# Up projection of a gated encoder block: products of a pair summed in one PSUM bank, next pair's first product moved forward

## The chip, the cores and the metric

The kernel runs on one core of a Trainium2 chip. The metric is device time in microseconds (us) of one execution. TensorE (PE) multiplies into PSUM banks; VectorE (DVE) and ScalarE (ACT) read PSUM; GpSimd (POOL) works on SBUF alone here; SyncE (SP) issues the DMAs. Each engine works through its own queue in order, and semaphores hold it until what it needs is done.

## The reference, cut to what matters

```python
h2 = _rmsnorm(x, norm2_g[l])
u = h2 @ ffn_up[l]                        # [2048, 1024] @ [1024, 5504]
u = cw[0] * _shift_prev(u) + cw[1] * u + cw[2] * _shift_next(u) + ffn_conv_b[l]
u_gate, u_val = jnp.split(u, 2, axis=-1)
x = x + (jax.nn.silu(u_gate) * u_val) @ ffn_down[l]
```

Everything ahead of this (two token mixers, merge, output projection) and behind it (down projection, last norm) is the same in both kernels. Float32 is needed all through, so a float32 factor is split into a high and a low part and a product takes three matmuls: high by high, high by low, low by high.

## The kernel before, in words

The up projection computes u transposed, channels on partitions and tokens along the row. The 5504 channels are 43 tiles of 128: 21 pairs of a gate tile and the value tile that goes with it, and one mixed tile of 64 and 64. The 2048 tokens go in two sweeps q = 0 and q = 1, of two blocks of 512 tokens each, so there are 42 pairs (line 1653 lists the steps; the mixed tile is the first step of sweep 0 and the last of sweep 1).

A pair is a product of 2 by 2 blocks: rows are the gate and the value tile, the inner index is the two halves of the 1024 inputs, columns are the two token blocks. It is done with seven block products in place of eight. On the weights' side stand A11, A12, A22 and the sums S1 to S4, on the activations' side B11, B21, B22 and the sums T1 to T4. `prod` (line 1491) does one block product: 4 slices of the inner index by 3 parts, 12 matmuls of 128x128 by 512 columns, into a bank of its own. `up_pair` (line 1620) calls it seven times, in the order A11·B11, S2·T2, S3·T3, S1·T1, A12·B21, A22·T4, S4·B22. ACT copies the first product into the tile row `ug` (line 1631); seven additions on DVE (`plus`, line 1498, a bank plus an SBUF row into an SBUF row) make the four quarters c11 and c12 (of `ug`) and c21 and c22 (of `uv`) out of it. Banks come from `bank()` (line 1574), eight in turn; `ug` and `uv` have two buffers each.

`pair_weights` (line 1550) makes the weights' side of the next pair while a pair runs. SP loads two raw tiles `rw` (line 1538), POOL forms the sums (line 1553, four of 128x512 a pair), ACT casts the high parts whi, s1h, s3h and s4h (line 226), and line 227 subtracts to get the low parts: wlo and s3l on POOL, s1l and s4l on DVE. The tiles whi and wlo have two buffers, the s tiles one each, so the next pair's S3 can be written only when A22·T4 of this pair is done. The raw tiles have four buffers, freed by s4l, s1l and s3l in turn.

`glu` (line 1602) is the convolution and gate of a pair that is finished: for two segments and both tiles one ACT operation (line 1597) and two DVE operations (lines 1598 and 1599), then SiLU on ACT (line 1605), a DVE multiplication (line 1607) and a DMA to `d_act`. It is called one step late, at the end of the loop at line 1656, through `pend`. `u_tile` and `u_done` move edge columns of the sweeps on POOL (lines 1585 to 1593).

In the last pair of sweep 0 (line 1662) the activations of sweep 1 replace those of sweep 0: `load_mat` (line 1541), called after each product, loads the operand that this product used last, through the single buffer `wraw` and the three buffers `ev`, and splits it anew. This stretch is called the turn below.

The order in each engine's queue is not written by hand: a scheduler lays it out at build time from a model of the durations, by priority, which is the order of the program; `tc.high_priority(300)` puts an instruction 300 places further ahead. On the chip this order is fixed.

Of the kernel before, what the change touches and what calls it, by code (L numbers as in the profile page):

```python
# [166 lines left out]
def _body(tc, A, out, dump=None, upto=99):  # L167
    nc = tc.nc
# [4 lines left out]
    def pool(stack, name, bufs=1, space=None, **kw):  # L173
        if space is None:
            return stack.enter_context(tc.tile_pool(name=name, bufs=bufs, **kw))
        return stack.enter_context(tc.tile_pool(name=name, bufs=bufs, space=space, **kw))
# [48 lines left out]
    def split(hi, lo, src, lo_eng=None, hi_eng=None):  # L225
        (hi_eng or nc.scalar.copy)(out=hi, in_=src)  # L226
        (lo_eng or nc.vector).tensor_tensor(out=lo, in0=src, in1=hi.bitcast(F32), op=ALU.subtract)  # L227
# [70 lines left out]
    def operand(b, q, **kw):  # L298
        t = [[q.tile([128, 4, BT], F32R, name=f"h{nm}{b}{i}", **kw) for nm in ("hi", "lo")] for i in range(2)]
        return [Halves([x[j] for x in t]) for j in range(2)]  # L300
# [3 lines left out]
    for b in range(NB):  # L304
        x_, y_ = operand(b, hb, **FOP) if b == NB - 1 else operand(b, hp)
# [93 lines left out]
    for b in range(NB):  # L399
        ps = pg.tile([128, 512], F32, name="pg", tag="pg")  # L400
# [3 lines left out]
        o = ev.tile([128, 512], F32, name="ev", tag="ev")  # L404
# [1007 lines left out]
    mats = {}  # L1412
# [12 lines left out]
    MATS = ("B11", "T2", "T3", "T1", "B21", "T4", "B22")  # L1425
# [64 lines left out]
    def prod(ps, *terms):  # L1490
        mm = [(w[ph == 2][:, k, :], x[ph == 1][:, k, :]) for w, x in terms for ph in range(3) for k in range(4)]
        for i, (w_, x_) in enumerate(mm):
            nc.tensor.matmul(ps, w_, x_, start=i == 0, stop=i == len(mm) - 1)  # L1493
        return ps

    def plus(o, ps, t):
        with tc.high_priority(300):
            nc.vector.tensor_tensor(out=o, in0=ps, in1=t, op=ALU.add)  # L1498

    def up_mixed(w, bank, u0, u1):  # L1500
        wh, wl = w
        a, b = (wh[:, 0:4], wl[:, 0:4]), (wh[:, 4:8], wl[:, 4:8])
        p1 = prod(bank(), (a, mats["B11"]))
        with tc.high_priority(300):
            nc.scalar.copy(out=u0, in_=p1)
        plus(u1, prod(bank(), (a, mats["T1"]), (b, mats["B22"])), u0)
        plus(u0, prod(bank(), (b, mats["B21"])), u0)
# [20 lines left out]
    fw = pool(s6, "fw", reuse_waits="tile")  # L1528
# [6 lines left out]
    def raw_tile(src):  # L1535
        r = fr.tile([128, 8, 128], F32, name="rw", tag="rw", bufs=4)
        if src is not None:
            sync.dma_start(out=f2(r), in_=src)
        return r

    def load_mat(n, i):
        r = wp.tile([128, 1024], F32, name="wraw", tag="wraw", bufs=1)
        sync.dma_start(out=r, in_=d_mat[i][:, 0:2, :].rearrange("p a b -> p (a b)"))
        split(f2(mats[n][0][:, 0:2, :]), f2(mats[n][1][:, 0:2, :]), r)
        for k in range(2, 4):
            r = ev.tile([128, BT], F32, name="ev", tag="ev")
            sync.dma_start(out=r, in_=d_mat[i][:, k, :])
            split(mats[n][0][:, k, :], mats[n][1][:, k, :], r, lo_eng=nc.gpsimd if k == 3 else nc.vector)

    def pair_weights(i):  # L1550
        r1, r2 = raw_tile(A["wup"][2 * i]), raw_tile(A["wup"][2 * i + 1])
        a, b = slice(0, 4), slice(4, 8)
        ps_ = lambda o, x, y, op: nc.gpsimd.tensor_tensor(out=o, in0=x, in1=y, op=op)  # L1553

        def parts(q, names, src, eng, n=8):
            h, l = [q.tile([128, n, 128], F32R, name=x, tag=x, bufs=2 if q is wp else 1) for x in names]
            split(f2(h), f2(l), f2(src), lo_eng=eng)
            return h, l

        h, l = parts(wp, ("whi", "wlo"), r1, nc.gpsimd)  # L1560
        w = {"A11": (h[:, a], l[:, a]), "A12": (h[:, b], l[:, b])}
        rs = raw_tile(None)
        ps_(rs[:, a], r2[:, a], r2[:, b], ALU.add)
        ps_(rs[:, b], rs[:, a], r1[:, a], ALU.subtract)
        h, l = parts(fw, ("s1h", "s1l"), rs, nc.vector)
        w["S1"], w["S2"] = (h[:, a], l[:, a]), (h[:, b], l[:, b])
        ps_(r2[:, a], r1[:, a], r2[:, a], ALU.subtract)
        h, l = parts(fw, ("s3h", "s3l"), r2, nc.gpsimd)
        w["S3"], w["A22"] = (h[:, a], l[:, a]), (h[:, b], l[:, b])
        ps_(r1[:, b], r1[:, b], rs[:, b], ALU.subtract)  # L1570
        w["S4"] = parts(fw, ("s4h", "s4l"), r1[:, b], nc.vector, 4)
        return w

    def bank():
        nbank[0] += 1
        return pus[(nbank[0] - 1) % 8 >= 3].tile([128, 512], F32, name="pu", tag="pu")


    COLS = ((slice(2, 514), slice(514, 1026)), (slice(1, 513), slice(517, 1029)))
    SEG = (((3, 511, 513), (514, 511, 1024)), ((1, 513, 0), (516, 513, 1535)))  # L1580

    def u_tile(q, m, tag):
        u = fu.tile([128, 1030], F32, name=tag, tag=tag, bufs=2)
        if q == 1:
            nc.gpsimd.memset(u[:, 0:1], 0.0)
            nc.gpsimd.tensor_copy(out=u[:, 513:517], in_=halo[:, m, :])
            nc.gpsimd.memset(u[:, 1029:1030], 0.0)
        return u

    def u_done(q, m, u):  # L1590
        if q == 0:
            nc.gpsimd.tensor_copy(out=halo[:, m, 0:2], in_=u[:, 2:4])
            nc.gpsimd.tensor_copy(out=halo[:, m, 2:4], in_=u[:, 1024:1026])

    def conv(m, u, c0, n):
        c = fc.tile([128, 513], F32, name="cv", tag="cv", bufs=6)[:, 0:n]
        nc.scalar.activation(out=c, in_=u[:, c0:c0 + n], func=AF.Identity, scale=vc("cw1", m), bias=vc("cb", m))  # L1597
        nc.vector.scalar_tensor_tensor(out=c, in0=u[:, c0 - 1:c0 - 1 + n], scalar=vc("cw0", m), in1=c, op0=ALU.mult, op1=ALU.add)  # L1598
        nc.vector.scalar_tensor_tensor(out=c, in0=u[:, c0 + 1:c0 + 1 + n], scalar=vc("cw2", m), in1=c, op0=ALU.mult, op1=ALU.add)  # L1599
        return c  # L1600

    def glu(q, i, ug, uv):
        for c0, n, t0 in SEG[q]:
            g = conv(2 * i, ug, c0, n)
            nc.scalar.activation(out=g, in_=g, func=AF.Silu)
            v = conv(2 * i + 1, uv, c0, n)
            nc.vector.tensor_tensor(out=v, in0=v, in1=g, op=ALU.mult)  # L1607
            sync.dma_start(out=d_act[i, :, t0:t0 + n], in_=v)
# [8 lines left out]
            sync.dma_start(out=d_act[21, 0:64, t0:t0 + n], in_=vm[0:64])  # L1617
            sync.dma_start(out=d_act[21, 64:128, t0:t0 + n], in_=vm[0:64])

    def up_pair(q, i, w, after):  # L1620
        ug, uv = u_tile(q, 2 * i, "ug"), u_tile(q, 2 * i + 1, "uv")
        c11, c12, c21, c22 = [u[:, c] for u in (ug, uv) for c in COLS[q]]

        def pr(a, b):
            ps = prod(bank(), (w[a], mats[b]))
            after(b)
            return ps

        p1 = pr("A11", "B11")
        with tc.high_priority(300):  # L1630
            nc.scalar.copy(out=c11, in_=p1)
        plus(c12, pr("S2", "T2"), c11)
        plus(c21, pr("S3", "T3"), c12)
        p5 = pr("S1", "T1")
        plus(c12, p5, c12)
        plus(c22, p5, c21)
        plus(c11, pr("A12", "B21"), c11)
        plus(c21, pr("A22", "T4"), c21)
        plus(c12, pr("S4", "B22"), c12)
        u_done(q, 2 * i, ug)  # L1640
        u_done(q, 2 * i + 1, uv)
        return lambda: glu(q, i, ug, uv)

    def mixed(q, w):
        u = u_tile(q, 42, "ug")
        if q == 0:
            nc.scalar.copy(out=u[:, 2:1026], in_=u42)
        else:
            up_mixed(w, bank, *[u[:, c] for c in COLS[q]])
        u_done(q, 42, u)  # L1650
        return lambda: glu_mixed(q, u)

    steps = [(0, 21)] + [(q, i) for q in range(2) for i in range(21)] + [(1, 21)]
    weights = lambda i: load_w(A["wup"][42]) if i == 21 else pair_weights(i)
    nw, pend = None, None
    for n, (q, i) in enumerate(steps):
        w = nw
        if n + 1 < len(steps):
            nw = weights(steps[n + 1][1])
        if n == 0:  # L1660
            load_mat("T4", 7)
        turn = q == 0 and i == 20
        if i == 21:
            fin = mixed(q, w)
        else:
            fin = up_pair(q, i, w, lambda b: load_mat(b, MATS.index(b)) if turn else None)
        if pend:
            pend()
        pend = fin
    pend()  # L1670
    s6.close()
# [97 lines left out]
    nx = prep_act(*work[0])  # L1769
    for tt in range(4):  # L1770
        fin = last_norm(tt, ps0[tt])
        next(fin)
        next(fin)
    for w, (tt, k0) in enumerate(work):
        ah, al = nx
        if k0 == 0:
            ps = banks(tt)
            fin = last_norm(tt, ps)
        if w + 1 < len(work):
            nx = prep_act(*work[w + 1])  # L1780
# [38 lines left out]
```

## Time and profile before

| | |
|---|---|
| median of 3 runs | 3625.32 us (3624.73 to 3634.07) |
| profiled execution, its own time | 3635.12 us |
| its span, first to last instruction | 3633.3 us |
| mean granted clock of TensorE | 0.956 |
| busy share of the span | PE 91%, DVE 64%, ACT 43%, POOL 28% |
| up projection, pairs and mixed tile | from about 2263 to 3140 us of the span |

The busy shares are means over stages with different limits. A matmul is recorded longer than the time by which it advances the next one, since they are pipelined; the pace of PE is read from starts of like instructions, and what holds it from the time that stands in brackets before an instruction.

### The profile page before, as it was taken

Reading aid. Unit: us, or ns where it says so; the run is one execution under the profiler, and the core shown is the slowest. Engines: PE = TensorE matmul, PEld = TensorE weight load, DVE = VectorE, ACT = ScalarE, POOL = GpSimd, SP = SyncE. Lnnn points to the kernel's source line nnn. Section 1 sums busy time; section 2 is a strip of 40 time slices with the busy share of each in tenths; the row PEclk is TensorE's granted clock in tenths of the full one; section 3 lists DMA queues with packets and bytes.
Section 4 is the critical chain, followed back from the end, with each engine's and each line's share of the span. In section 5 each row is a group of like instructions: output and inputs, shape, how many; then the busy total and the mean of one; then the engine's idle time right before and its main releaser. Section 6 shows DMA issues by size and latency. Waiting matters only on the chain. (4 is left out here: it accounts for less than half of the span.)

```text
span 3633.3 us, 58213 instructions
## 1 busy us (share of the span) xinstructions
PE 3291.2 (91%) x22232; PEld 2622.3 (72%) x22232; DVE 2319.6 (64%) x3913; ACT 1569.8 (43%) x2870; POOL 1003.0 (28%) x789
## 2 busy tenths in 40 slices
PE   7999999998978878877767899999989999999999
PEld 6787778766657666666655788877768777778887
DVE  5207764688846665666766466989899989724222
ACT  4214443555546666666544333434344443511111
POOL 1122222244430000000024412676766666100000
PEclk9999999999988999998988999999989999999999
DMA  4233444688883545555788746322232222523222
GB/s 148 91 118 109 134 137 134 197 224 229 230 247 108 158 151 158 153 182 177 216 244 271 286 140 199 115 76 79 78 125 96 81 76 82 168 86 115 83 83 64
DMA packets 403223, 531.30 MB, mean 146 GB/s; under 512 B 61504, under 2 KB 250560, under 8 KB 402944
## 3 DMA queue, kind: packets, MB, share of 16 engines
q1 hardware_dynamic: 402944, 527.58, 46.5%
q8 instruction: 175, 2.87, 0.3%
q14 instruction: 104, 0.85, 0.1%
HBM read 345.02 MB, written 181.93 MB: 145 GB/s over the span
## 5 line engine op out<-in xcount | busy, mean ns | idle before, releaser
L1553 POOL TENSOR_TENSOR rw<-rw 128x512 f32<-128x512 f32 x168 | 274.4, 1653 | 4.6 <-DVE cv L1598 1.2
L1706 PE MATMUL pd<-wdh,whi 128*128 128x512 f32 x672 | 261.6, 391 | 1.6 <-DVE ug L1498 1.6
L1707 PE MATMUL pd<-wdl,whi 128*128 128x512 f32 x672 | 261.4, 389 | 0.0
L1708 PE MATMUL pd<-wdh,wlo 128*128 128x512 f32 x672 | 259.3, 389 | 0.0
L241 PE MATMUL pg<-hhi,whi 128*128 128x512 f32 x928 | 249.0, 403 | 3.1 <-ACT whi L226 3.1
L241 PE MATMUL pg<-hlo,whi 128*128 128x512 f32 x928 | 250.5, 402 | 0.0
L241 PE MATMUL pg<-hhi,wlo 128*128 128x512 f32 x928 | 248.7, 403 | 0.0
L1073 POOL TENSOR_TENSOR Lt<-Lt,rnr 128x512 f32<-128x512 f32 x16 | 19.4, 1234 | 824.9 <-DVE rnr L254 766.5
L241 PEld LDWEIGHTS pg<-hhi,whi 128*128 128x128 f32 x928 | 176.2, 192 | 54.4 <-issue 14.3
L241 PEld LDWEIGHTS pg<-hhi,wlo 128*128 128x128 f32 x928 | 176.1, 192 | 49.8 <-issue 13.6
L241 PEld LDWEIGHTS pg<-hlo,whi 128*128 128x128 f32 x928 | 174.0, 191 | 52.4 <-issue 17.5
L227 POOL TENSOR_TENSOR wlo<-wraw,whi 128x1024 fp32r<-128x1024 f32 x46 | 114.9, 2498 | 349.6 <-PE pg L241 157.8
L1213 PE MATMUL pf<-fop,whi 128*128 128x512 f32 x576 | 172.6, 438 | 39.1 <-ACT whi L226 23.6
L1597 ACT ACTIVATE cv<-ug,vec 128x511 f32<-128x511 f32 (+1 forms) x88 | 71.9, 817 | 249.5 <-DVE ug L1498 249.5
L226 ACT CAST whi<-wraw 128x1024 fp32r<-128x1024 f32 x114 | 119.3, 1046 | 114.3 <-PE pg L241 50.8
L1213 PEld LDWEIGHTS pf<-fop,whi 128*128 128x128 f32 x576 | 113.7, 207 | 71.6 <-ACT whi L226 28.5
L1695 ACT CAST whi<-wraw 128x1024 fp32r<-128x1024 f32 (+1 forms) x36 | 35.2, 979 | 265.9 <-PE pd L1707 180.5
L1706 PEld LDWEIGHTS pd<-wdh,whi 128*128 128x128 f32 x672 | 126.1, 188 | 30.7 <-issue 5.0
L1598 DVE SCALAR_TENSOR_TENSOR cv<-ug,vec,cv 128x511 f32<-128x511 f32 (+1 forms) x88 | 125.0, 1421 | 35.8 <-ACT cv L1597 35.8
L227 DVE TENSOR_TENSOR wlo<-wraw,whi 128x1024 fp32r<-128x1024 f32 x68 | 83.7, 1231 | 99.4 <-ACT whi L226 98.8
L1708 PEld LDWEIGHTS pd<-wdh,wlo 128*128 128x128 f32 x672 | 126.2, 188 | 26.2
L1707 PEld LDWEIGHTS pd<-wdl,whi 128*128 128x128 f32 x672 | 126.2, 188 | 25.6
(470 smaller groups left out, 8274.4 us busy)
## 6 DMA issues: line engine op xcount, KB each, us to landing
rw<-wup SPq DMA_DIRECT2D x84, 512.0 KB, 3.5
wraw<-win SPq DMA_DIRECT2D x74, 512.0 KB, 4.1
Lt<-d_lt SPq DMA_DIRECT2D x64, 512.0 KB, 5.6
d_lt<-arbk SPq DMA_DIRECT2D x96, 256.0 KB, 3.9
d_gate<-ev SPq DMA_DIRECT2D x64, 256.0 KB, 3.5
X<-d_vt SPq DMA_DIRECT2D x64, 256.0 KB, 4.6
bj<-d_lt SPq DMA_DIRECT2D x128, 128.0 KB, 3.9
d_m<-ev SPq DMA_DIRECT2D x64, 256.0 KB, 5.4
```

The source lines that it names most:

```text
L226: (hi_eng or nc.scalar.copy)(out=hi, in_=src)
L227: (lo_eng or nc.vector).tensor_tensor(out=lo, in0=src, in1=hi.bitcast(F32), op=ALU.subtract)
L241: nc.tensor.matmul(ps, (wh, wh, wl)[ph], (xh, xl, xh)[ph], start=(ph == 0 and i == 0), stop=(ph == 2 and i == n - 1))
L1073: nc.gpsimd.tensor_tensor(out=y8[t], in0=y8[t], in1=b8(rr[:, t * 8:t * 8 + 8]), op=ALU.mult)
L1213: nc.tensor.matmul(ps, (wh, wh, wl)[ph][:, k0 + k, :], (hi, lo, hi)[ph][:, k, :], start=i == first[u] and k == 0, stop=i == last[u] and k ...
L1553: ps_ = lambda o, x, y, op: nc.gpsimd.tensor_tensor(out=o, in0=x, in1=y, op=op)
L1597: nc.scalar.activation(out=c, in_=u[:, c0:c0 + n], func=AF.Identity, scale=vc("cw1", m), bias=vc("cb", m))
L1598: nc.vector.scalar_tensor_tensor(out=c, in0=u[:, c0 - 1:c0 - 1 + n], scalar=vc("cw0", m), in1=c, op0=ALU.mult, op1=ALU.add)
L1695: nc.scalar.copy(out=ah[:, 0:n], in_=raw[:, 0:n])
L1706: nc.tensor.matmul(ps, a, wdh[k][:, cs], start=(k == 0), stop=False)
L1707: nc.tensor.matmul(ps, a, wdl[k][:, cs], start=False, stop=False)
L1708: nc.tensor.matmul(ps, l, wdh[k][:, cs], start=False, stop=False)
```

## The change

`up_pair` sums the partial sums in the bank. Bank X takes A11·B11, then S2·T2, S1·T1 and S4·B22 on top of it, and after each of the four ACT copies what X then holds: c11, c21, c22 and c12. Bank Y takes S3·T3 and later A22·T4; Z takes A12·B21. Three DVE additions are left: Y to c22, Z to c11, Y to c21. The first product of a pair and its copy (`up_head`) are called from the pair before, between A12·B21 and A22·T4 (`mid`), and so is the convolution of the pair before that (`pend`). The low part s3l is made on DVE.

```diff
-        h, l = parts(fw, ("s3h", "s3l"), r2, nc.gpsimd)
+        h, l = parts(fw, ("s3h", "s3l"), r2, nc.vector)
...
+    def add_to(ps, w, x, first=False):
+        mm = [(w[ph == 2][:, k, :], x[ph == 1][:, k, :]) for ph in range(3) for k in range(4)]
+        for n, (w_, x_) in enumerate(mm):
+            nc.tensor.matmul(ps, w_, x_, start=first and n == 0, stop=n == len(mm) - 1, skip_group_check=True)
+
+    def taken(o, ps):
+        with tc.high_priority(300):
+            nc.scalar.copy(out=o, in_=ps)
+
+    def up_head(q, i, w, after):
         ug, uv = u_tile(q, 2 * i, "ug"), u_tile(q, 2 * i + 1, "uv")
+        X = bank()
+        add_to(X, w["A11"], mats["B11"], True)
+        after("B11")
+        taken(ug[:, COLS[q][0]], X)
+        return ug, uv, X
+
+    def up_pair(q, i, w, after, st, mid):
+        ug, uv, X = st
         c11, c12, c21, c22 = [u[:, c] for u in (ug, uv) for c in COLS[q]]
...
-        p1 = pr("A11", "B11")
-        with tc.high_priority(300):
-            nc.scalar.copy(out=c11, in_=p1)
-        plus(c12, pr("S2", "T2"), c11)
-        plus(c21, pr("S3", "T3"), c12)
-        p5 = pr("S1", "T1")
-        plus(c12, p5, c12)
-        plus(c22, p5, c21)
-        plus(c11, pr("A12", "B21"), c11)
-        plus(c21, pr("A22", "T4"), c21)
-        plus(c12, pr("S4", "B22"), c12)
+        pr(X, "S2", "T2")
+        taken(c21, X)
+        Y = bank()
+        pr(Y, "S3", "T3", True)
+        pr(X, "S1", "T1")
+        taken(c22, X)
+        Z = bank()
+        pr(Z, "A12", "B21", True)
+        plus(c22, Y, c22)
+        plus(c11, Z, c11)
+        nx = mid()
+        pr(Y, "A22", "T4")
+        plus(c21, Y, c21)
+        pr(X, "S4", "B22")
+        taken(c12, X)
...
+    def between(n):
+        if pend:
+            pend()
+        if n + 1 < len(steps) and steps[n + 1][1] < 21:
+            return up_head(*steps[n + 1], nw, afters(n + 1))
...
         if i == 21:
             fin = mixed(q, w)
+            st = between(n)
         else:
-            fin = up_pair(q, i, w, lambda b: load_mat(b, MATS.index(b)) if turn else None)
-        if pend:
-            pend()
+            fin, st = up_pair(q, i, w, afters(n), st, lambda: between(n))
         pend = fin
```

## Rows read from the trace of the kernel before

**Rows 1.** Busy time by stretch: 16 pairs, the turn's 2, then 4, then 15 pairs

```profile
core 0: us, PE busy (x) PEld busy (x) DVE busy (x) ACT busy (x) POOL busy (x), PEclk, DMA share, GB/s
2360.37:2684.48 324.11, 310.88 (x1345) 249.87 (x1344) 293.53 (x303) 130.43 (x178) 226.46 (x164) 1.00 0.23 78
2684.48:2750.56 66.08, 49.20 (x169) 36.71 (x168) 59.93 (x57) 32.78 (x44) 40.90 (x38) 0.79 0.50 162
2750.56:2826.72 76.16, 76.16 (x337) 63.06 (x336) 70.24 (x77) 30.56 (x41) 49.59 (x50) 1.00 0.26 87
2826.72:3127.65 300.93, 290.48 (x1262) 235.18 (x1260) 271.89 (x290) 123.50 (x166) 183.27 (x173) 1.00 0.24 77
```

**Rows 2.** Timeline: end of a pair's last product on PE, its addition on DVE

```profile
2302.34 1.07 PE L1493 MATMUL pu<-mB22h,s4l 128*128 128x512 f32 x4
...
2309.78 0.68 DVE L1498 TENSOR_TENSOR ug<-pu,ug 128x512 f32<-128x512 f32 x1
...
2340.42 1.07 PE L1493 MATMUL pu<-mB22h,s4l 128*128 128x512 f32 x4
...
2350.37 0.68 DVE L1498 TENSOR_TENSOR ug<-pu,ug 128x512 f32<-128x512 f32 x1
...
2501.12 1.07 PE L1493 MATMUL pu<-mB22h,s4l 128*128 128x512 f32 x4
...
2512.60 0.68 DVE L1498 TENSOR_TENSOR ug<-pu,ug 128x512 f32<-128x512 f32 x1
```

**Rows 3.** Who waited for whom, 2400 to 2660 us: total, times, longest

```profile
ACT cv L1597 <- DVE ug L1498: 93.3, 26, 3.7
...
ACT cv L1605 <- DVE cv L1599: 45.4, 12, 3.8
DVE cv L1598 <- ACT cv L1597: 23.0, 26, 0.9
...
PE pu L1493 <- POOL s3l L227: 10.9, 13, 0.9
```

**Rows 4.** Timeline of one pair in sweep 0: how s3l comes late

```profile
2498.40 1.07 PE L1493 MATMUL pu<-mT4h,s3l 128*128 128x512 f32 x4
...
2506.32 1.03 ACT L226 CAST s3h<-rw 128x1024 fp32r<-128x1024 f32 x1
...
2507.91 2.38 POOL L227 TENSOR_TENSOR s3l<-rw,s3h 128x1024 fp32r<-128x1024 f32 x1
...
2510.34 1.20 PE L1493 MATMUL pu<-mT3h,s3l 128*128 128x512 f32 x4 [0.84 <-POOL s3l L227]
...
2513.80 0.74 DVE L1599 SCALAR_TENSOR_TENSOR cv<-ug,vec,cv 128x511 f32<-128x511 f32 x1
2513.88 5.21 POOL L1553 TENSOR_TENSOR rw<-rw 128x512 f32<-128x512 f32 x3
...
2514.46 1.78 DVE L1598 SCALAR_TENSOR_TENSOR cv<-ug,vec,cv 128x511 f32<-128x511 f32 x1
```

**Rows 5.** Groups by shape over ten pairs of sweep 0, 2400 to 2602.7 us

```profile
L1498 DVE TENSOR_TENSOR ug<-pu,ug 128x512 f32<-128x512 f32 x40 | 27.3, 683 | 1.0
L227 POOL TENSOR_TENSOR s3l<-rw,s3h 128x1024 fp32r<-128x1024 f32 x10 | 23.8, 2380 | 0.0
L227 DVE TENSOR_TENSOR s1l<-rw,s1h 128x1024 fp32r<-128x1024 f32 x10 | 12.2, 1216 | 0.0
L1631 ACT COPY ug<-pu 128x512 f32<-128x512 f32 x10 | 5.7, 565 | 0.0
```

**Rows 6.** The same groups in sweep 1, ten pairs, 2866.5 to 3067.34 us

```profile
L227 DVE TENSOR_TENSOR s1l<-rw,s1h 128x1024 fp32r<-128x1024 f32 x10 | 23.4, 2342 | 0.0
```

**Rows 7.** Timeline of the turn: B11's first cast, PE's longest wait, the last operand

```profile
2677.01 1.04 ACT L226 CAST mB11h<-wraw 128x1024 fp32r<-128x1024 f32 x1
...
2712.92 2.07 PE L1493 MATMUL pu<-mT1l,s1h 128*128 128x512 f32 x4 [7.29 <-DVE mT1l L227]
...
2732.29 2.70 DVE L227 TENSOR_TENSOR mB22l<-wraw,mB22h 128x1024 fp32r<-128x1024 f32 x1 [0.20 <-ACT mB22h L226]
```

**Rows 8.** Who waited for whom in sweep 1, 2800 to 3080 us

```profile
ACT cv L1605 <- DVE cv L1599: 86.8, 28, 5.5
```

More of the change, by code (lines that the diff above doesn't have):

```diff
@@ L1618, in glu_mixed, with pr @@
             sync.dma_start(out=d_act[21, 64:128, t0:t0 + n], in_=vm[0:64])
-    def up_pair(q, i, w, after):
-        ug, uv = u_tile(q, 2 * i, "ug"), u_tile(q, 2 * i + 1, "uv")
+    def add_to(ps, w, x, first=False):
[6 more added lines that the diff above has]
+    def up_head(q, i, w, after):
+        ug, uv = u_tile(q, 2 * i, "ug"), u_tile(q, 2 * i + 1, "uv")
+        X = bank()
[5 more added lines that the diff above has]
+        ug, uv, X = st
         c11, c12, c21, c22 = [u[:, c] for u in (ug, uv) for c in COLS[q]]
-        def pr(a, b):
-            ps = prod(bank(), (w[a], mats[b]))
+        def pr(ps, a, b, first=False):
+            add_to(ps, w[a], mats[b], first)
             after(b)
-            return ps
-        p1 = pr("A11", "B11")
-        with tc.high_priority(300):
-            nc.scalar.copy(out=c11, in_=p1)
-        plus(c12, pr("S2", "T2"), c11)
-        plus(c21, pr("S3", "T3"), c12)
-        p5 = pr("S1", "T1")
-        plus(c12, p5, c12)
-        plus(c22, p5, c21)
-        plus(c11, pr("A12", "B21"), c11)
-        plus(c21, pr("A22", "T4"), c21)
-        plus(c12, pr("S4", "B22"), c12)
+        pr(X, "S2", "T2")
[13 more added lines that the diff above has]
+        taken(c12, X)
         u_done(q, 2 * i, ug)
         u_done(q, 2 * i + 1, uv)
-        return lambda: glu(q, i, ug, uv)
+        return (lambda: glu(q, i, ug, uv)), nx
     def mixed(q, w):
@@ L1654, in _body, with afters @@
     weights = lambda i: load_w(A["wup"][42]) if i == 21 else pair_weights(i)
-    nw, pend = None, None
+    nw, pend, st = None, None, None
+    def afters(n):
+        turn = steps[n] == (0, 20)
+        return lambda b: load_mat(b, MATS.index(b)) if turn else None
+    def between(n):
[3 more added lines that the diff above has]
+            return up_head(*steps[n + 1], nw, afters(n + 1))
     for n, (q, i) in enumerate(steps):
@@ L1661, in _body @@
             load_mat("T4", 7)
-        turn = q == 0 and i == 20
         if i == 21:
             fin = mixed(q, w)
+            st = between(n)
         else:
-            fin = up_pair(q, i, w, lambda b: load_mat(b, MATS.index(b)) if turn else None)
-        if pend:
-            pend()
+            fin, st = up_pair(q, i, w, afters(n), st, lambda: between(n))
         pend = fin
```

## The prediction

> **What bounds the kernel now.** I read the busy time by stretch first. In the four pairs after the turn PE is busy all the time, and a pair takes 76.16 / 4 = 19.04 us [rows 1]. That is PE's floor, since the change keeps the seven products of 12 matmuls; one product is 19.04 / 7 = 2.72 us. The 16 pairs of the first long stretch take 20.26 us each and the 15 of the last 20.06 us [rows 1], so 16 x 1.22 + 15 x 1.02 = 19.5 + 15.3 = 34.8 us lie above the floor. The turn with its two pairs takes 66.08 us, 28.0 above.
>
> What makes the difference is seen in the timeline [rows 2]. A pair's last product ends on PE at 2303.41 us (start plus duration) and is added on DVE 6.4 us later; two pairs on the delay is 8.9 us, and at 2502 us it is 10.4. Between the first two of these PE made two pairs in 38.08 us and DVE in 40.59. So DVE runs its own circuit of 20.3 us whether PE is ahead or not, PE ran ahead as far as the buffers allow, and then took DVE's pace. In that circuit DVE is busy 293.53 / 16 = 18.35 us [rows 1] and waits 23.0 / 13 = 1.77 us for ACT's convolution operation [rows 3].
>
> The table of waits then shows where PE feels it: at s3l, up to 0.9 us a pair on the matmul itself [rows 3]. The chain in one pair [rows 4]: A22·T4 ends at 2499.47, but ACT casts s3h only at 2506.32, because it stands in its queue behind a convolution that waits up to 3.7 us for a DVE addition [rows 3]; POOL needs 2.38 us for s3l, and PE waits for its end. The late s3l is a symptom of a late DVE.
>
> **The change part by part.**
>
> *Additions to copies.* Seven additions become three: 4 x 0.683 = 2.73 us leave DVE a pair [rows 5]. ACT makes four copies in place of one, 3 x 0.565 = 1.70 us [rows 5]; it goes from 130.43 / 16 = 8.15 to 9.85 us of a 19.04 us pair. As load that is free; its place in the queue is the second rival.
>
> *s3l on DVE.* 2.38 us leave POOL [rows 5], whose load falls from 14.15 to 11.8 us a pair. DVE's price for the same shape is s1l: 1.22 us in sweep 0 [rows 5], 2.34 in sweep 1 [rows 6]; these are also the bounds, and I take each sweep's own. Freed POOL time helps DVE: the same kind of convolution operation takes 0.74 us beside an idle POOL and 1.78 beside a busy one [rows 4]. A 2.38 us s3l can hit none or two of them, so the relief lies between 0 and 2.1 us; I take 1.0.
>
> DVE's circuit becomes 20.26 - 2.73 + 1.22 - 1.0 = 17.8 us in sweep 0 and 20.06 - 2.73 + 2.34 - 1.0 = 18.7 in sweep 1. The dearest case is 20.26 - 2.73 + 2.34 = 19.9, the cheapest 16.4. Below 19.04 PE sets the pace, and the 34.8 us go.
>
> The Trainium skill (SBUF — State Buffer, Who interferes with whom) has VectorE instructions with two SBUF inputs and GpSimd instructions that read SBUF exclude each other for a whole instruction. The 0.74 and 1.78 us rows [rows 4] agree. By that rule s3l, which has two SBUF inputs, still takes its turn against POOL from the other side, and the circuit would stand at the dear end, the first rival.
>
> *One bank for four products.* X may be added to only after ACT has copied it. Between S2·T2 and S1·T1 stands one product, so c21's copy has 2.72 - 0.565 = 2.15 us to spare. c22's copy has three products or more of cover. c11's has two (A22·T4 and S4·B22 of the pair before) but needs a free buffer of `ug`, so the convolution of the pair before last must be done; DVE's former delay of 10.4 us is no longer affordable, and with DVE below the floor it does not build up. Y is read twice by DVE, with three products between its two fillings. I cost these waits together at 0.25 us a pair, between 0 and 1.0: 31 x 0.25 = 8 us.
>
> *What the moved head and convolution bring along.* The head's 12 matmuls pass A22·T4 and S4·B22 on PE. That takes 2.72 us from the time for the new S3: from the end of A22·T4 to S3·T3 there were three products, 8.16 us, now two, 5.44. s3h came 6.85 us late and lasts 1.03 [rows 4]; unchanged, it would cost PE 2.4 us a pair. I cost it at nothing, because the ACT wait that delayed it was for a late DVE addition. On POOL the head's edge columns wait for a free `ug`, and the next pair's sums queue behind them; the 2.38 us taken off POOL cover that. On SP the convolution's two stores stand earlier and wait for their multiplications, with the raw weight loads behind; those run a pair ahead. Costed at nothing; without that cover they would come out at PE like a late s3h.
>
> *The turn.* Seven operands pass one buffer, from B11's cast at 2677.01 to the end of B22's at 2734.99 [rows 7], 8.3 us each, with PE waiting up to 7.29 us for one. B11's three DMAs, casts and subtractions are now called two products, 5.4 us, ahead of the rest of the last pair, so the series may start that much sooner. B11 is also wanted two products sooner. I take -5 us, between -10 and +8. The first pair of all has no product between its head and S2·T2: +1 us.
>
> *Sum.* -19.5 - 15.3 + 8 - 5 + 1 = -31 us. The profiled execution took 3635.1 us, so 3604; the median of the runs stands 9.8 us below it, so 3594 on its level.
>
> **The rivals.**
>
> *DVE stays the bound.* s3l costs 2.34 us everywhere and relieves nothing: a circuit of 19.9 us gains 0.4 us a pair, 31 x 0.4 = 12 us in all and nothing in the turn: 3613. For it speaks the dear s1l of sweep 1; against it, s1l at 1.22 in sweep 0 in every one of ten pairs.
>
> *PE waits for ACT (slower).* The queue on ACT is fixed at build time, and a copy of X can come to stand behind a SiLU that waits for DVE's last convolution operation: 3.8 us once a pair in sweep 0 [rows 3], up to 5.5 in sweep 1 [rows 8]. Less the 2.15 us to spare, that is 1.7 to 3.4 us of idle PE a pair, and a late s3h would cost 2.4 in the same manner. At 2.4 us over 40 pairs it is 96 - 34.8 - 5 = +56 us: 3681. It decides from 40 / 40 = 1.0 us a pair on; below that the change still gains. For it: today each product has a bank of its own, and eight banks absorbed 10 us of delay that X cannot. Against it: those waits are long because DVE is late, and its load falls by a tenth.
>
> The Trainium skill (PSUM — Partial Sum Buffer, PSUM bank collisions raise a hardware error) says that TensorE must not write a bank while another engine reads it. Thus a copy in the middle of a sum is always time that X is closed to PE. No run here shows such a copy yet; by that rule alone this rival has its mechanism.
>
> *The order is not as written.* The scheduler may leave the head behind S4·B22. Then S2·T2 follows A11·B11 in the same bank, every pair waits for a copy of 0.565 us and two handoffs, some 1 us, and the gain is eaten: 3625.
>
> **How the numbers follow.** Forecast 0.52, DVE still the bound 0.18, PE waiting for ACT 0.18, order 0.12. The predicted time is the forecast's 3594 us. Its own range, with waits of 0 to 0.6 us a pair and the turn from -10 to +8, is 3580 to 3618. The whole range reaches from 3576 to 3638: the upper end takes in both middle cases and stalls of up to 1.3 us a pair, and leaves out most of the slower case. A measurement of this kernel can tell some 0.3%, 11 us, from no change. The first rival lies on that line and is halved; of the last one a quarter goes to slower: faster 0.61, same 0.18, slower 0.21.
>
> **What the profile would show.** If right: starts of like matmuls 19.04 to 19.3 us apart in both sweeps, no PE wait for s3l, DVE's busy share below 95% of a pair with three additions and one s3l more, additions on DVE within some 5 us of their product. The first rival would show a pair above 19.7 us with DVE without idle time. The second would show PE waiting ahead of S1·T1 or S2·T2 for ACT's copy, or ahead of S3·T3 for s3h, and under that row ACT waiting for DVE. The third would show A11·B11 directly ahead of S2·T2. The prediction is wrong if PE's idle time a pair is above 1 us, or if the turn costs over 8 us more.

## The result and the profile after

The changed kernel takes 3647.07 us (median of 4 runs, 3646.54 to 3650.16) against 3627.57 us (3624.73 to 3634.07) for the kernel before in the same series: a ratio of 1.0053 [1.0036, 1.007] (behind a ratio stand the ends of its 95% interval). The forecast was 3594 us with a range up to 3638. So the change made the kernel 0.5% slower where the forecast had it faster.

The profiled execution spans 3648.3 us at a mean granted clock of 0.953, against 3633.3 us at 0.956. Of these +15.0 us, 13.6 lie in the up projection: from its first matmul to the first of the down projection it takes 876.9 us before and 890.5 after. PE's floor for its 3576 matmuls, by the 19.04 us for the 84 matmuls of a pair [rows 1], is 3576 x 19.04 / 84 = 810.6 us.

The first part of the page, after:

```profile
PE 3296.5 (90%) x22232; PEld 2631.5 (72%) x22232; DVE 2233.4 (61%) x3787; ACT 1637.4 (45%) x2996; POOL 903.8 (25%) x747
```

The work went where it was meant to go: DVE's share fell from 64 to 61%, POOL's from 28 to 25%, ACT's rose from 43 to 45%. DVE is no longer the bound, and the time is longer all the same. Busy time by stretch, after: eight pairs of sweep 0, eight of sweep 1, and 3.51 us out of the first stretch, from where PE resumes after a long wait.

```profile
core 0: us, PE busy (x) PEld busy (x) DVE busy (x) ACT busy (x) POOL busy (x), PEclk, DMA share, GB/s
...
2411.65:2575.44 163.79, 155.33 (x673) 127.12 (x672) 127.80 (x129) 78.46 (x112) 90.31 (x72) 0.98 0.24 78
...
2915.79:3079.76 163.97, 156.23 (x673) 127.50 (x672) 131.32 (x129) 78.38 (x113) 84.34 (x89) 0.98 0.24 78
...
2514.99:2518.50 3.51, 3.51 (x8) 2.80 (x9) 1.80 (x2) 0.43 (x1) 0.18 (x1) 0.50 0.49 141
```

672 matmuls are eight pairs, so a pair takes 163.79 / 8 = 20.47 us in sweep 0 and 20.50 in sweep 1, where it took 20.26 and 20.06 before [rows 1]. DVE is busy 127.80 / 8 = 16.0 us of it, which leaves it 4.5 us idle a pair. PE is idle for 163.79 - 155.33 = 8.46 us in the eight pairs, and over these 3.51 us its granted clock is 0.50, the lower of its two levels (1.2 GHz).

Who PE waited for, after, from 2260 to 3160 us (total us, times, longest):

```profile
PE pu L1624 <- ACT s1h L226: 29.5, 10, 7.3
PE pu L1624 <- ACT ug L1628: 6.4, 1, 6.4
PE pu L1624 <- ACT uv L1628: 4.2, 4, 1.7
PE pu L1624 <- ACT s3h L226: 3.5, 1, 3.5
```

The waits for s3l [rows 3] are gone. In their place stand a few long waits for ACT. Five of them, of 6.05 to 7.26 us, come one in every eight pairs (at 2351, 2515, 2680, 2855 and 3019 us), always ahead of S2·T2, and half clock follows each. The third falls in the turn. One of them in the timeline, after:

```profile
2498.62 1.05 ACT L226 CAST s3h<-rw 128x1024 fp32r<-128x1024 f32 x1 [5.81 <-issue]
...
2499.49 0.69 DVE L1498 TENSOR_TENSOR uv<-pu,uv 128x512 f32<-128x512 f32 x1 [4.70 <-PE pu L1624]
...
2501.83 1.78 DVE L1598 SCALAR_TENSOR_TENSOR cv<-uv,vec,cv 128x511 f32<-128x511 f32 x1
...
2503.62 5.20 POOL L1553 TENSOR_TENSOR rw<-rw 128x512 f32<-128x512 f32 x3
...
2504.20 1.78 DVE L1599 SCALAR_TENSOR_TENSOR cv<-uv,vec,cv 128x511 f32<-128x511 f32 x1
...
2505.90 1.78 DVE L1598 SCALAR_TENSOR_TENSOR cv<-ug,vec,cv 128x511 f32<-128x511 f32 x1
...
2507.60 1.77 DVE L1598 SCALAR_TENSOR_TENSOR cv<-uv,vec,cv 128x511 f32<-128x511 f32 x1
2507.67 1.07 PE L1624 MATMUL pu<-mT1h,s1l 128*128 128x512 f32 x4
2508.78 2.79 POOL L227 TENSOR_TENSOR wlo<-rw,whi 128x1024 fp32r<-128x1024 f32 x1
2509.29 2.82 DVE L1598 SCALAR_TENSOR_TENSOR cv<-ug,vec,cv 128x511 f32<-128x511 f32 x1
2512.04 0.74 DVE L1599 SCALAR_TENSOR_TENSOR cv<-ug,vec,cv 128x511 f32<-128x511 f32 x1
...
2512.89 0.59 ACT L1628 COPY ug<-pu 128x512 f32<-128x512 f32 x1 [6.47 <-DVE cv L1599]
...
2513.37 0.63 ACT L1605 ACTIVATE cv<-cv 128x511 f32<-128x511 f32 x1
...
2513.90 1.03 ACT L226 CAST s1h<-rw 128x1024 fp32r<-128x1024 f32 x1
...
2514.99 2.07 PE L1624 MATMUL pu<-mT2h,s1h 128*128 128x512 f32 x4 [6.24 <-ACT s1h L226]
```

S1 and S2 lie in one tile, s1h, that has one buffer. Here PE's queue has the next pair's S2·T2 directly behind S1·T1, so the cast of s1h can begin only when S1·T1 ends, at 2508.74 us. That alone would cost PE the cast, 1.03 us. ACT comes to the cast only at 2513.90, 5.2 us later: in its queue stand, ahead of it, the head's copy of c11, which waits 6.47 us for a free buffer of `ug`, and a SiLU. The buffer is freed by DVE's last convolution operation at L1599, and DVE is late. It was idle for 4.70 us until PE delivered A22·T4. ACT, which has the first step of the convolution behind the cast of s3h, was idle for 5.81 us: s3h has one buffer too, and the cast starts 0.08 us after A22·T4's last read of it (2498.54; the profile names no releaser). DVE then ran the convolution beside a busy POOL: four operations of 1.77 to 1.78 us and one of 2.82, where their like takes 0.74 (at 2512.04). That is 6.2 us more than five times 0.74. So DVE and ACT idle for PE, and then PE idles for DVE, by way of ACT.

That PE has S2·T2 there is the other half. The order of the products in the built queues (12 matmuls each, a number behind the colon where a product was cut up) is, before, the same in every pair but the first and those of the turn, and after, for example:

```
before  A11·B11  S2·T2  S3·T3  S1·T1  A12·B21  A22·T4  S4·B22
after   S4 A22 S2 S3:8 A12:8 S3:4 A12:4 S1 A11:23 S4:6 A22 S4:6 S2 A11:1 ...
```

Before, 48 matmuls stand between S1·T1 and the next pair's S2·T2, at 38 of the 41 places (43, 4 and 76 at the start and in the turn). After, it is any number from 0 to 68. In sweep 0 a pattern of eight pairs repeats, 60, 35, 47, 9, 2, 62, 20, 0, and sweep 1 has nearly the same. The five zeros of the 41 are the five long waits.

### The profile page after: what moved, and what is told of

The parts are those of the page before. It is cut to its first block, busy times and chain, and to the rows that moved or that the text cites. A ratio compares the mean times of both kernels' runs of the same rounds, so it can differ in the third digit from the quotient of the medians.

```text
span 3648.3 us, 58052 instructions
## 1 busy us (share of the span) xinstructions
PE 3296.5 (90%) x22232; PEld 2631.5 (72%) x22232; DVE 2233.4 (61%) x3787; ACT 1637.4 (45%) x2996; POOL 903.8 (25%) x747
## 5 line engine op out<-in xcount | busy, mean ns | idle before, releaser
L1073 POOL TENSOR_TENSOR Lt<-Lt,rnr 128x512 f32<-128x512 f32 x16 | 19.9, 1267 | 824.1 <-DVE rnr L254 782.0
L1728 DVE TENSOR_TENSOR wlo<-wraw,whi 128x1024 fp32r<-128x1024 f32 (+1 forms) x36 | 39.3, 1091 | 150.8 <-ACT whi L1725 150.8
L1598 DVE SCALAR_TENSOR_TENSOR cv<-ug,vec,cv 128x511 f32<-128x511 f32 (+1 forms) x88 | 113.0, 1284 | 21.8 <-ACT cv L1597 21.8
```

The costliest lines, as they stand in the source:

```text
L1728: nc.vector.tensor_tensor(out=al[:, 0:m], in0=raw[:, 0:m], in1=ah[:, 0:m].bitcast(F32), op=ALU.subtract)
```

## Experiments

Each was run beside the kernel before, which takes 3634.6 to 3636.9 us in these series, where it took 3627.57 above. So runs of different series are compared by their ratios. Theory A of the expectations has the chain just shown decide, with the busy `ug` buffer at its head; theory B has DVE's crowded queue make ACT late anyway; theory C has the short covers between S1·T1 and S2·T2 cost time by themselves.

### The buffer: e1_cv5 and e2_ug3

A third buffer of `ug` has no room unless the convolution's tiles give up one of six. So e1 takes one of these away alone, as the control, and e2 gives the room to `ug` (the other line that asks for a `cv` tile is changed alike).

```diff
-        c = fc.tile([128, 513], F32, name="cv", tag="cv", bufs=6)[:, 0:n]
+        c = fc.tile([128, 513], F32, name="cv", tag="cv", bufs=5)[:, 0:n]
...
-        u = fu.tile([128, 1030], F32, name=tag, tag=tag, bufs=2)
+        u = fu.tile([128, 1030], F32, name=tag, tag=tag, bufs=3 if tag == "ug" else 2)
```

> The changed kernel with five convolution tiles in place of six; the order of every engine's queue is the same. It is the control for the run with three ug buffers, which needs the room. Every theory: as the changed kernel, 3647 us within 6, with the five long PE idles of 6.0 to 7.3 us ahead of S2·T2. If the sixth tile mattered, it comes out slower by more than 10 us.

> As the control, with three buffers for ug in place of two. Theory A (ACT's c11 copy of the moved head waits for the ug buffer of the pair before last, s1h stands behind it in ACT's queue, PE waits 6.0 to 7.3 us for it five times and then runs at the lower clock for some 3 us more): the five idles fall below 1 us, 5 x 9 = 45 us less than the control, 3595 to 3610. Theory B (the rest of DVE's crowded queue, with s3l in it, makes s1h or the copy late anyway): the idles stay above 4 us, 3635 to 3650. Theory C (the order of products on PE costs the time): no more than 10 us less than the control.

e1: 3660.72 us, ratio 1.0073 [1.0058, 1.0088]. e2: 3645.16 us, 1.0026 [1.0016, 1.0037]. The control missed its expectation: it takes 13.7 us more than e3 below, which is the changed kernel but for one priority and ran in the same series, so the sixth tile matters. The buffer gives back 15.6 us against the control, much less than the 45 us that theory A expected, and little more than the tile had cost. The same place in the timeline of e2:

```profile
2501.28 0.58 ACT L1628 COPY ug<-pu 128x512 f32<-128x512 f32 x1
...
2509.66 0.63 ACT L1605 ACTIVATE cv<-cv 128x511 f32<-128x511 f32 x1 [6.33 <-DVE cv L1599]
2510.20 1.03 ACT L226 CAST s1h<-rw 128x1024 fp32r<-128x1024 f32 x1
2511.28 2.08 PE L1624 MATMUL pu<-mT2h,s1h 128*128 128x512 f32 x4 [5.69 <-ACT s1h L226]
```

The copy of c11 no longer waits. The SiLU behind it now waits 6.33 us for the very same DVE operation, and s1h stands behind the SiLU. Theory A falls in its narrow form, and the time lies in theory B's range: the buffer is one of two things in ACT's queue that wait for a late DVE.

### The copy's place on ACT: e3_noprio

```diff
-        taken(ug[:, COLS[q][0]], X)
+        nc.scalar.copy(out=ug[:, COLS[q][0]], in_=X)
```

> The changed kernel with the c11 copy of the head at its own priority, so that it no longer stands 300 places ahead in ACT's queue. Theory A: s1h may pass it, but S2·T2 still needs the copy, which waits for the buffer; each of the five idles gets 1 to 2 us shorter, 3635 to 3647. If the queue's order alone were to blame (A in its narrow form), the idles go: 3600 to 3615. Theory C: 3647 within 6.

3647.07 us, 1.0038 [1.0024, 1.0053]. PE still waits 29.3 us for s1h (9 times, up to 7.2). The high priority of that one copy is not what matters.

### One part alone: e4_b_s3dve

The kernel before, with s3l on DVE and nothing else; PE's order stays.

```diff
-        h, l = parts(fw, ("s3h", "s3l"), r2, nc.gpsimd)
+        h, l = parts(fw, ("s3h", "s3l"), r2, nc.vector)
```

> The kernel before, with s3l on VectorE and nothing else; the order on PE is all but the same. If the first rival of the prediction holds (s3l on VectorE costs DVE its full price, DVE is the bound): DVE's circuit grows by 1.2 to 2.3 us less 0 to 2.1 of relief, 0 to +1.5 us a pair over 42 pairs, 3627 to 3690. If POOL's s3l as such was what PE waited for: 1 us a pair less, 3590 to 3600.

3601.16 us (3599.58 to 3603.95), 0.9909 [0.9892, 0.9925]: 33 us faster, with one word changed. That is 1 us above the range for POOL's s3l as what PE waited for, and far below the first rival's. Starts of like matmuls in sweep 0, a long window of it and nine pairs late in sweep 1, all in e4; then DVE groups over ten pairs of sweep 0, before and in e4:

```profile
2495.27 1.07 PE L1493 MATMUL pu<-mB11h,whi 128*128 128x512 f32 x4
...
2514.31 1.07 PE L1493 MATMUL pu<-mB11h,whi 128*128 128x512 f32 x4
```

```profile
2360.00:2680.00 320.00, 316.00 (x1386) 259.84 (x1384) 301.75 (x334) 141.79 (x191) 213.88 (x158) 1.00 0.28 91
...
2908.00:3085.00 177.00, 174.68 (x757) 140.37 (x756) 167.75 (x181) 73.86 (x99) 90.19 (x99) 1.00 0.24 78
```

```profile
L1598 DVE SCALAR_TENSOR_TENSOR cv<-ug,vec,cv 128x511 f32<-128x511 f32 x20 | 32.5, 1624 | 8.9 <-ACT cv L1597 8.9
L1598 DVE SCALAR_TENSOR_TENSOR cv<-uv,vec,cv 128x511 f32<-128x511 f32 x20 | 32.2, 1611 | 8.8 <-ACT cv L1597 8.8
```

```profile
L1598 DVE SCALAR_TENSOR_TENSOR cv<-uv,vec,cv 128x511 f32<-128x511 f32 x20 | 25.1, 1257 | 0.0
...
L1598 DVE SCALAR_TENSOR_TENSOR cv<-ug,vec,cv 128x511 f32<-128x511 f32 x20 | 22.1, 1105 | 8.9 <-ACT cv L1597 8.9
...
L227 DVE TENSOR_TENSOR s3l<-rw,s3h 128x1024 fp32r<-128x1024 f32 x10 | 12.1, 1209 | 0.0
```

In sweep 0 a pair takes 19.04 us, PE's floor. DVE got s3l on top, 1.21 us a pair, and yet is busy 301.75 / 320 x 19.04 = 17.95 us of a pair, less than its 18.35 before [rows 1]: 18.35 + 1.21 - 17.95 = 1.6 us came back as other DVE operations got faster with POOL out of the way, above all L1598, whose mean for `ug` fell from 1624 to 1105 ns. DVE also waits less: of its two waits for ACT's convolution operation in a pair, some 0.9 us each, the one ahead of `uv` is gone, since s3l now runs in that time.

In sweep 1 the floor is not held to the end: the nine pairs shown take 177.00 / 9 = 19.67 us each, with DVE busy for 95% of it and waiting for ACT for most of the rest. There DVE is the bound again.

### Order and parts: e5_order, e6_order_s3pool, e7_s3pool, e8_nohead

e5 is the changed kernel with each product tied in PE's queue behind the last matmul of the product that is called before it. The work is the same. The scheduler lays out the other queues anew as well, from the same model.

```diff
+    last_mm = [None]
...
-        for n, (w_, x_) in enumerate(mm):
-            nc.tensor.matmul(ps, w_, x_, start=first and n == 0, stop=n == len(mm) - 1, skip_group_check=True)
+        with ExitStack() as st_:
+            if last_mm[0] is not None:
+                st_.enter_context(tc.issue_after(last_mm[0]))
+            for n, (w_, x_) in enumerate(mm):
+                nc.tensor.matmul(ps, w_, x_, start=first and n == 0, stop=n == len(mm) - 1, skip_group_check=True)
+        last_mm[0] = nc.cur_bb.bb.instructions[-1]
```

> The changed kernel with the products held on PE in the order of the program (issue order only, no added wait): four products between S1·T1 of a pair and S2·T2 of the next, everywhere, where the changed kernel has between 0 and 68 matmuls and five places with 0. Theory C (the five long idles are these five places: S1 has one buffer, so its cast starts only after S1·T1 and has nothing to hide behind): pairs 19.04 to 19.4 us apart, no idle above 2 us outside the turn, 25 to 40 us below the kernel before. Theory A (ACT's queue waits for DVE's late convolution, whatever the order on PE): idles of 2 us or more ahead of S1·T1, S2·T2 or S3·T3 in most pairs, not below the kernel before. The turn may cost up to 10 us more than now, since PE can no longer go around a late operand.

3599.25 us (3593.78 to 3604.26), 0.9906 [0.9888, 0.9924]. Between S1·T1 and the next S2·T2 there are 48 matmuls again. Starts, busy time and PE's longest waits in e5:

```profile
2491.17 1.07 PE L1629 MATMUL pu<-mB11h,whi 128*128 128x512 f32 x4
...
2510.24 1.07 PE L1629 MATMUL pu<-mB11h,whi 128*128 128x512 f32 x4
```

```profile
2360.00:2640.00 280.00, 280.00 (x1235) 231.60 (x1234) 242.96 (x233) 149.57 (x206) 173.80 (x134) 1.00 0.26 83
```

```profile
PE pu L1629 <- ACT uv L1634: 4.4, 2, 2.3
PE pu L1629 <- DVE mB21l L227: 4.2, 1, 4.2
```

19.07 us a pair, PE without idle time, DVE busy 242.96 / 280 x 19.04 = 16.5 us. The waits for s1h are gone with no buffer added. The stage takes 834.6 us, 55.9 less than in the changed kernel. In that one all waits of PE in the stage sum to 54.2 us against 14.5 in e5; part of the rest is the lower clock behind each long wait, 3.51 / 2 = 1.8 us in the window shown. ACT's queue differs too: in e5 c11's copy (at 2494.16) stands ahead of the convolution's SiLUs. ACT still waits 2.95 us for DVE ahead of the SiLU before s1h, but four products lie between and PE does not feel it. So the run shows that the order as built matters; it does not part PE's queue from ACT's.

e6 is e5 with s3l on POOL; e7 is the changed kernel with s3l on POOL, in the order of the scheduler. Both have `nc.gpsimd` in the line of e4's diff. e8 is the changed kernel with the head called in its own pair:

```diff
-        if n + 1 < len(steps) and steps[n + 1][1] < 21:
-            return up_head(*steps[n + 1], nw, afters(n + 1))
...
-            fin, st = up_pair(q, i, w, afters(n), st, lambda: between(n))
+            fin, st = up_pair(q, i, w, afters(n), up_head(q, i, w, afters(n)), lambda: between(n))
```

> The same with s3l back on POOL: the sums in one bank and the moved head alone, in the order of the program. If the fewer additions were enough to free DVE (20.26 - 2.73 = 17.5 us, below 19.04), it is 15 to 35 us below the kernel before. If s3l on POOL still comes late (the time for the new S3 is 5.4 us in place of 8.2, and s3l is 2.4 us long on POOL), a wait for it of 1 to 3 us shows in each pair: 0 to 70 us above the kernel before.

> The changed kernel with s3l back on POOL and the scheduler's own order, which again has places without a matmul between S1·T1 and S2·T2. With s3l on DVE being worth 33 us in the kernel before, theories that let the parts add up say 3647 + 33 = 3680. If the fewer additions already give what s3l on DVE gives, the two don't add up: 3640 to 3655.

> The changed kernel with the head in its own pair, so that S2·T2 is written right behind A11·B11 in the same bank. The scheduler's order again has six places without a matmul between S1·T1 and the next S2·T2. Theory C: long idles at these places, within 15 us of the changed kernel. If the moved head were the cause of the loss, this gives 3600 to 3625.

e6: 3622.39 us, 0.9969 [0.9957, 0.998]. e7: 3711.27 us, 1.0213 [1.0195, 1.0231]. e8: 3692.59 us, 1.0167 [1.0146, 1.0188].

So in a strict order the sums and the moved head together give 0.3%, about 11 us where the expectation had at least 15, with no wait for s3l left, and s3l brings the rest. In the scheduler's order s3l on DVE is worth about 60 us (e7 against the changed kernel), and both expectations were too low. PE waits 36.8 us for s1h in e7, so lateness reaches PE there. In e6 a pair takes 19.8 us, and what PE waits for is copies of X:

```profile
PE pu L1629 <- ACT uv L1634: 15.9, 21, 4.6
PE pu L1629 <- DVE uv L1498: 4.1, 15, 0.3
```

e8 was expected near the changed kernel and is over 40 us slower, with 20.4 us of PE waiting for the copy of c11. In this order the moved head is no cause of the loss; it helps.

### One edge, or other banks: e9_s2behind_s4 and e10_banks

e9 ties S2·T2 alone behind the S4·B22 of the pair before, which turns the five zeros into twelves. e10 leaves the order to the scheduler, and takes X always from the first of the two pools of banks (three), Y and Z from the second (five), where the changed kernel takes all eight in turn, three a pair.

```diff
+    last_mm = [None]
...
-        pr(X, "S2", "T2")
+        with ExitStack() as st_:
+            if last_mm[0] is not None:
+                st_.enter_context(tc.issue_after(last_mm[0]))
+            pr(X, "S2", "T2")
...
+        last_mm[0] = nc.cur_bb.bb.instructions[-1]
```

```diff
+    def xbank():
+        return pus[0].tile([128, 512], F32, name="pu", tag="pu")
+
+    def ybank():
+        return pus[1].tile([128, 512], F32, name="pu", tag="pu")
...
-        X = bank()
+        X = xbank()
...
-        Y = bank()
+        Y = ybank()
...
-        Z = bank()
+        Z = ybank()
```

> The changed kernel with one tie alone: S2·T2 of a pair is issued behind S4·B22 of the pair before; the other products stay where the scheduler puts them. The five places with 0 matmuls between S1·T1 and S2·T2 get 12, 2.7 us. If the idle is s1h's delay less what lies between (theory C), each of the five idles of 6.0 to 7.3 us shrinks by about 2.7 us to 3.3 to 4.6: 13 to 25 us below the changed kernel. If it is the general disorder of the products, the idles move elsewhere: within 8 us of the changed kernel.

> The changed kernel with X always from the pool of three banks and Y and Z from the pool of five, in place of all from eight in turn. In sweep 0 the scheduler then repeats one order in every pair, not with S2·T2 as far from S1·T1 as in the program but 10 matmuls, 2.3 us, and A22·T4 6 matmuls from the next S3·T3. If the turning of eight banks by three a pair makes the irregular order and that makes the loss: at most 15 us above the kernel before in sweep 0 and the long idles gone. Theory C: s1h and s3h come after 1.2 us at the least, more where ACT waits, so a short cover in each of 20 pairs costs 0.5 to 3 us each: 3640 to 3690.

e9: 3640.61 us (3635.3 to 3648.32), 1.0021 [1.001, 1.0031]. The wait moved to the product that now stands first, and to the copy it needs. At three of the five places it has the same length (6.2 to 7.3 us); at the other two it is split, 2.0 and 2.7 us at one, 2.1 and 2.4 at the other. The first of the three, and the sum:

```profile
2508.68 2.07 PE L1626 MATMUL pu<-mB22h,s4h 128*128 128x512 f32 x4 [6.22 <-ACT uv L1630]
```

```profile
PE pu L1626 <- ACT uv L1630: 34.6, 14, 7.3
```

At these three ACT is late, whichever product comes next. The time does not decide between the expectation's branches (6.5 us below the changed kernel by the medians, 12 by the ratios); these rows speak for the second.

e10: 3591.43 us (3589.81 to 3599.01), 0.9889 [0.9871, 0.9906], below both kernels. Its order in sweep 0 repeats in every pair, but with only 10 matmuls between S1·T1 and the next S2·T2. Starts, busy time, PE's longest wait and the c11 copy with s1h in e10:

```profile
2489.51 1.07 PE L1630 MATMUL pu<-mT2h,s1h 128*128 128x512 f32 x4
...
2508.55 1.07 PE L1630 MATMUL pu<-mT2h,s1h 128*128 128x512 f32 x4
```

```profile
2360.00:2640.00 280.00, 280.00 (x1237) 231.84 (x1236) 210.26 (x235) 149.88 (x210) 173.84 (x133) 1.00 0.26 81
```

```profile
PE pu L1630 <- ACT s1h L226: 4.6, 1, 4.6
```

```profile
2504.74 0.59 ACT L1634 COPY ug<-pu 128x512 f32<-128x512 f32 x1 [0.79 <-DVE cv L1605]
2505.22 0.64 ACT L1611 ACTIVATE cv<-cv 128x511 f32<-128x511 f32 x1
2505.76 1.05 ACT L226 CAST s1h<-rw 128x1024 fp32r<-128x1024 f32 x1
```

Copy, SiLU and cast stand in the same order as at the long idle of the changed kernel. Here the copy waits 0.79 us in place of 6.47, because DVE is done with the convolution operation that frees the buffer. The expectation of theory C, that a short cover costs something each time, missed: 10 matmuls are 2.27 us, the cast takes 1.05, and PE loses nothing as long as ACT is free. The one that put the loss down to the turning banks held.

### Do they add up: e11_banks_order and e12_banks_s3pool

e11 is e10 with the edges of e5; e12 is e10 with s3l on POOL.

> Both mends in one: products in the program's order and X in banks of its own. If the order on PE and the turning banks are two sides of one cause, the two don't add up: within 8 us of the better of the two runs, 0.987 to 0.992 of the kernel before. If each mends something of its own, 8 to 15 us less than either: 0.984 to 0.987.

> X in banks of its own with s3l back on POOL: the sums in one bank and the moved head without the third part. The scheduler's order repeats every three pairs, with 8 to 14 matmuls between S1·T1 and S2·T2. If short covers are harmless as long as DVE has time to spare (17.5 us of 19.04 by the prediction's sum), 0.990 to 1.000 of the kernel before; if s3l on POOL takes that time and makes ACT late, the long idles come back: 1.005 to 1.025.

e11: 3593.42 us, 0.9883 [0.9868, 0.9898], the same as e10. The two do not add up; as each alone brings the pairs to PE's floor, this does not tell one cause from two. e12: 3741.84 us, 1.0284 [1.0265, 1.0303], the slowest of all, beyond the branch of its expectation in which the long idles come back. Busy time and PE's waits in e12:

```profile
2400.00:2640.00 240.00, 205.34 (x848) 165.66 (x848) 175.30 (x150) 98.90 (x141) 136.20 (x101) 0.94 0.20 66
```

```profile
PE pu L1630 <- ACT s1h L226: 51.2, 12, 5.7
PE pu L1630 <- ACT whi L226: 47.7, 24, 3.4
```

The short covers that were free in e10 go with a PE that is idle for 240.00 - 205.34 = 34.7 us, a seventh of the stretch. They are not the cause; they are what turns lateness on DVE and ACT into idle time on PE.

## Why the prediction was wrong

**The floor and the bound** were read rightly. Below DVE's pace lies PE's 19.04 us: e5 and e10 reach it, and e4 in sweep 0, each in another way.

**s3l on DVE** was priced at 1.22 us in sweep 0, and e4 shows 1.21; the 2.34 us for sweep 1 did not come, it is 1.22 there too. The relief was taken at 1.0 us and is 1.6 in e4's sweep 0. It was read from a row that does not say it: POOL was not idle beside the 0.74 us operation but started 0.08 us after it (2513.88 against 2513.80) [rows 4]. The first rival (19.9 us a pair and no relief) is refuted in sweep 0 by the same run; in sweep 1 of e4 DVE is the bound, at 19.67. And the split was wrong: the prediction let the additions bring 2.73 us of DVE's circuit and left to s3l a loss of 0.2 us. s3l alone brings most of the gain (e4: the stage takes 842.8 us where it took 876.9, and 834.5 in e5), sums and head alone a third of it (e6).

**The step that failed** is the one by which PE runs the products in the order in which the program calls them. All its covers were counted so: "between S2·T2 and S1·T1 stands one product", and for c11's copy "two (A22·T4 and S4·B22 of the pair before)". The third rival held the opposite, with a chance of 0.12, but pictured one regular misplacement at the price of no change. What came was an order that differs from pair to pair for eight pairs, in which products are cut up and the next S2·T2 lands directly behind S1·T1 once. In the order as called (e5) the forecast is met: 3594 / 3625.32 = 0.991 was forecast, 0.9906 [0.9888, 0.9924] is measured. That it is met so closely is in part luck: in the profiled executions the stage is 42.4 us shorter in e5 than before, where the sum had 31, since its waits outside the turn come to some 1 us in place of 8 and the turn gives 11 in place of 5.

**The term that was mis-sized with it** is the waits for copies and casts, 31 x 0.25 = 8 us. The row of s1h alone shows 29.5 us and all waits in the stage 54.2, and the lower clock behind the long ones comes on top. The prediction had named the weak link, that c11's copy needs a free `ug` and so a finished convolution, and set it aside with the words that DVE's delay would not build up. It does not build up over pairs; it comes up anew where the order makes DVE idle for 4.70 us and hands it the rest of the convolution beside a busy POOL. This is the second rival's mechanism, with a chance of 0.18: not 2.4 us in each pair, but 6 to 7 in one of eight. The sign of the result is that rival's; its time, 3681, is 34 us too high.

**The turn** was taken at -5 us. In e5 its three pairs take 74.1 us, 17.0 above the floor where 28.0 were: -11, one us beyond the range given.

**The signs.** No wait for s3l was left, as forecast. PE's idle time of 8.46 / 8 = 1.06 us a pair is the mark that the prediction itself had set for being wrong.

What stays open: why the scheduler's order turns irregular with eight banks in turn was not seen inside the scheduler. 24 banks are eight pairs of three, which fits the period, and e10 removes both the period in sweep 0 and the loss; but in sweep 1 of e10 the order is irregular again (10, 5, 38, 41 and 7 matmuls) without long idles. Whether DVE's idle time for Y or the crowding beside POOL decides in the long idle was not tried apart either: by the rows shown they come to 4.70 and 6.2 us, and either is of the size of PE's wait. Nor was it tried whether PE's order alone, with ACT's and DVE's left as they were, is enough.

## What to carry to other kernels

Before pricing a change to a kernel whose queues a scheduler orders, price the order too: how many products stand between the last reader of a single-buffered operand and its next use, in each pair of a full period, not in the program's text. When several long waits of one engine fall on different causes with one length, mending the last link can move the wait and leave its length (e2, three of five places in e9); mend the order (e5) or the rotation of the banks (e10). Try the smallest part of a change alone: here one word, s3l's engine, was worth 33 us, and the rest of the change, in its best order, some 8 to 9 us more of the stage (842.8 us in e4, 834.5 in e5, 833.4 in e10).

## What the runs showed of the hardware

The same DVE work costs very different time by what POOL is doing when it starts. e5 and e10 do the same DVE and POOL work in the same 280 us (POOL busy 173.8 in both), with DVE busy 242.96 against 210.26 us. Two of the groups that make this up, for e5 and then for e10:

```profile
L1599 DVE SCALAR_TENSOR_TENSOR cv<-uv,vec,cv 128x511 f32<-128x511 f32 x29 | 35.4, 1220 | 0.5
L227 DVE TENSOR_TENSOR s4l<-rw,s4h 128x512 fp32r<-128x512 f32 x15 | 26.7, 1780 | 0.0
```

```profile
L1605 DVE SCALAR_TENSOR_TENSOR cv<-uv,vec,cv 128x511 f32<-128x511 f32 x29 | 21.4, 738 | 0.0
...
L227 DVE TENSOR_TENSOR s4l<-rw,s4h 128x512 fp32r<-128x512 f32 x15 | 10.4, 692 | 36.9 <-PE pu L1630 36.9
```

s4l takes 1780 ns in the one and 692 in the other, with the same shape. These two groups are 30.3 of the 32.7 us. I had priced s3l by the rows of one order, and the order moves such prices by more than a factor of two.

The traces show what sets the price. Every s4l in e5 starts 1.2 us before the end of a tensor operation that POOL is at, every one in e10 while POOL is at none. So it is with the convolution's DVE operations, 460 in the stretches of five runs (before, after, e4, e5, e10): one that starts while a tensor operation runs on POOL lasts until that ends, and 0.54 to 0.56 us more; any other lasts 0.73 to 0.75 us, also where POOL starts one in the middle of it. In e10 POOL pays instead: its wlo takes 3.29 us on average, 2.40 in e5, and POOL has the time to spare.

The Trainium skill (SBUF — State Buffer, Who interferes with whom) has VectorE instructions with two SBUF inputs and GpSimd instructions that read SBUF exclude each other; the 692 against 1780 ns agree with it.

The long waits cost more than their length: where PE resumes after 6.24 us, its granted clock is 0.50 over the 3.51 us of the window at 2514.99 above, and the first four matmuls take 2.07 us in place of 1.07.
